# Cumulative sums along a diagonal: the sums of the last rows moved to TensorE, and the last places split over two PSUM tiles

## The chip, the cores and the metric

The kernel runs on one core of one Trainium2 chip. The metric is the device time of one execution in microseconds (us). Executions of the same kernel here spread over some 3.5 us (667.1 to 670.6), so differences of a few tenths of a microsecond are read from profiles, which time each instruction, and the timed runs tell only whether anything large has moved.

## The reference

```python
B, H, W = 4, 4224, 4224
x = randn(B, H, W).astype(float32)
ps = cumsum(cumsum(x, axis=1), axis=2)
diag = diagonal(ps, axis1=1, axis2=2)
out = cumsum(diag, axis=1).astype(float32)      # 4 x 4224
```

Each of the four matrices is read once (285 MB in all). The diagonal's element i is the sum of the leading (i+1) x (i+1) square, so it takes only row and column sums of the blocks on and beside the diagonal, and short scans of 384 places (11 groups make 4224).

## The kernel before

For each matrix, strips of 768 rows are loaded and converted to bf16. TensorE adds up columns into d (11 groups x 384), VectorE (DVE) and ScalarE (ACT) add up rows. The last matrix is treated apart, so that little is left to do when its last bytes land: the last group's rows come last, as part a (256 rows) in two loads, and part b (128 rows) in quarters, the last quarter in two loads. d and the scan of its groups are finished in the meantime. The sums of the last rows become places 0 to 383 of the last group (the code calls the row yl) by fp32 matmuls with a triangle of weights into the PSUM tile fin, called the weighing below; the last 32 places (ye) wait for the last quarter. In the code, arows are the sums of part a's rows, bsum those of the second and third quarter of part b, esum those of the last quarter; pu are the totals of d's groups, and carry is what each group adds from those before it.

Three helpers: `act_sum` adds up columns on ACT, `row_sums` and `pair_sum` on DVE, and `fold_in` lets TensorE add blocks of w columns into one PSUM tile by an identity matrix. The places concerned, at the last matrix:

```python
        for q in range(F2):
            matmul(d[:, q : GW : F2], r6[:, :NG, q], halves)
        for q in range(F):
            matmul(d[:, q : GW : F], r3[:, :, q], ident)

        if not whole:

            strip = strip_tile()
            part_a = strip[:, 0:2]
            part_b = strip[:, 2, :TB].rearrange("p (s c) -> p s c", s=4)
            acuts = [(1536, N - HC), (0, 1536)]
            for c0, c1 in acuts:
                nc.gpsimd.dma_start(out=part_a[:, :, c0:c1], in_=src_a[:, :, c0:c1])
            CB = TB // 4
            bcut = 768
            for sb, c0, c1 in (
                (0, 0, CB),
                (1, 0, CB),
                (2, 0, CB),
                (3, 0, bcut),
                (3, bcut, CB),
            ):
                r0 = TB + sb * R
                nc.gpsimd.dma_start(
                    out=part_b[:, sb, c0:c1],
                    in_=x[b, r0 : r0 + R, :TB].rearrange("r (k c) -> r k c", k=4)[
                        :, :, c0:c1
                    ],
                )

            fold_a = psum_s.tile([P, 2, 256], FP32, name="fold_a")
            c0, c1 = acuts[0]
            cp, ca = c0 + 768, c0 + 768 + 1152
            fold_in(fold_a, part_a, c0, cp, 256, start=True)
            for h in range(2):
                act_sum(asum[:, h, 1:2], part_a[:, h, cp:ca])
            row_sums(asum[:, :, 2], part_a[:, :, ca:c1])

        pu = smalls.tile([NG, 2], FP32, name="pu")
        c12 = smalls.tile([NG, 2, GW], FP32, name="c12")
        row_sums(pu[:, 0:1], d)
        masked(c12[:, 1, :], d, to_end, pu[:, 1:2])
        earlier, apart = order_whole if whole else order_last
        carry_ps = psum_s.tile([NG, 2], FP32, name="carry_ps")
        matmul(carry_ps, earlier, pu, start=True)
        matmul(carry_ps[:, 1:2], apart, pu[:, 0:1])
        carry = smalls.tile([NG, 2], FP32, name="carry")
        nc.vector.tensor_copy(out=carry, in_=carry_ps)
        for i, src in enumerate((d, c12[:, 0, :])):
            nc.vector.tensor_tensor_scan(
                out=c12[:, i, :],
                data0=ones_row,
                data1=src,
                initial=carry[:, i : i + 1],
                op0=ALU.mult,
                op1=ALU.add,
            )
        # ... store of groups 0 to 9; for the other matrices the loop ends here ...
        c0, c1 = acuts[1]
        cp = c0 + 768
        fold_in(fold_a, part_a, c0, cp, 256)
        for h in range(2):
            act_sum(asum[:, h, 3:4], part_a[:, h, cp:c1])
        row_sums(asum[:, :, 4], fold_a)
        arows = last.tile([P, 2], FP32, name="arows")
        row_sums(arows, asum)


        M0 = 2 * P
        E0 = GW - R
        fin = psum_s.tile([1, GW], FP32, name="fin")
        fin_e = psum_s.tile([1, R], FP32, name="fin_e")
        yl = last.tile([1, GW], FP32, name="yl")

        def weigh(rows, w, r0, start=False):

            matmul(fin[:, r0:], rows, w[:, : GW - r0], start=start)

        def finish(c0, c1):
            nc.vector.tensor_add(
                out=yl[:, c0:c1], in0=fin[:, c0:c1], in1=c12[0:1, 1, c0:c1]
            )

        by_ps = psum_s.tile([P, P], FP32, name="fold")
        for c in range(0, CB, P):
            matmul(by_ps, part_b[:, 0, c : c + P], weights4_h, start=c == 0)
        by = last.tile([P, P], FP32, name="by")
        nc.scalar.copy(out=by, in_=by_ps)
        weigh(dtot, weights, M0, start=True)
        weigh(ones_col, by, M0)
        weigh(arows[:, 0:1], weights, 0)
        weigh(arows[:, 1:2], weights, P)


        bsum = last.tile([P, 2, 2], FP32, name="bsum")
        for k, ca in ((0, 512), (1, 448)):
            act_sum(bsum[:, k, 0:1], part_b[:, k + 1, :ca])
            pair_sum(bsum[:, k, 1:2], part_b[:, k + 1, ca:])
        finish(0, M0)
        for k in range(2):
            for i in (1, 0):
                weigh(bsum[:, k, i : i + 1], weights4, M0 + (k + 1) * R)


        esum = last.tile([P, 3], FP32, name="esum")
        act_sum(esum[:, 0:1], part_b[:, 3, :320])
        pair_sum(esum[:, 1:2], part_b[:, 3, 320:bcut])
        pair_sum(esum[:, 2:3], part_b[:, 3, bcut:])
        for k in (1, 0, 2):
            matmul(fin_e, esum[:, k : k + 1], weights4[:, :R], start=k == 1)
        finish(M0, GW)
        nc.sync.dma_start(
            out=out[b, T0 : T0 + E0].unsqueeze(0), in_=yl[:, :E0]
        )
        ye = last.tile([1, R], FP32, name="ye")
        nc.vector.tensor_add(out=ye, in0=fin_e, in1=yl[:, E0:])
        nc.sync.dma_start(out=out[b, T0 + E0 : N].unsqueeze(0), in_=ye)
```

## Time and profile before

| | before |
|---|---|
| time, median of the first 3 runs | 667.89 us (667.13 to 668.78) |
| span of the profiled execution | 666.5 us |
| first columns of the last quarter landed (ACT starts on them) | 662.36 us |
| last store issued | 664.49 us |
| end of the span | 666.45 us |

Lines of the page's slices are tenths of busy time in 40 slices of the span. A timeline line is: start, duration, engine, line of the kernel, operation, output<-input, shapes, and in brackets the idle time of the engine before it and what ended that. The lines are shown in the prediction.

The granted clock is the profile's figure for TensorE, as a share of full speed. In the traces before and after it is 0.50 (half, also called cold) or 1.00 (full, warm) in each of 195 stretches of 3.41 us, and changes only between them; in the other traces the stretches asked for show the same two values. These stretches are called windows. The same four matmuls took 2.15 us at 0.50 (before) and 1.24 at 1.00 (b_again). Where the end of the program falls on this grid, the phase, differs from one execution to the next: the same kernel rose to full clock 3.37 us after the start of its last strip's fold in one (before) and 5.85 us in another (b_again).

One quantity carries this document: **the tail**, from the start of ACT's sum of 128x320, which begins as soon as the first columns of the last quarter have landed, to the issue of the last store. Before it is 664.49 - 662.36 = 2.13 us.

### The profile page before, as it was taken

What the parts mean: (1) busy time and instruction counts of PE and PEld (TensorE: products, weight loads), DVE (VectorE), ACT (ScalarE), POOL (GpSimd) and SP (SyncE); (2) the same over time, 40 slices, a digit from 0 to 9 for tenths busy, and PEclk for the clock granted to TensorE, in tenths of its full rate; (3) what the DMA queues carried; (4) which work ended last, traced back from release to release, by engine and by line L of the source; (5) the groups of instructions that cost most, each with busy time, mean ns of one, the idle gap of its engine ahead of it and who ended that gap; (6) DMA issues with size and microseconds to landing.
All of it is one profiled execution on the core that took longest, in us unless ns stands there. A gap on an engine that the chain in (4) does not pass through costs nothing.

```text
span 666.5 us, 2562 instructions
## 1 busy us (share of the span) xinstructions
PE 207.6 (31%) x981; PEld 98.5 (15%) x981; DVE 334.7 (50%) x165; ACT 140.3 (21%) x226; POOL 31.3 (5%) x59
## 2 busy tenths in 40 slices
PE   0081522403107154140321633504022254250426
PEld 0030211101103021010110311201011122120203
DVE  3160625446916153453882434537298334362866
ACT  0000120406300103040630020304063002030436
POOL 7000000000000000000000000000000000001000
PEclk9995857666558586665655957567565585765758
DMA  9999999999999999999999999999999999999997
GB/s 203 219 219 219 219 218 219 219 219 211 208 218 219 218 217 219 218 219 218 219 218 209 216 219 219 217 213 219 219 218 219 217 212 218 219 220 211 214 211 150
DMA packets 7670, 143.23 MB, mean 215 GB/s; under 512 B 702, under 2 KB 1002, under 8 KB 2154
## 3 DMA queue, kind: packets, MB, share of 16 engines
q0 software_dynamic: 7296, 142.47, 99.8%
q1 hardware_dynamic: 362, 0.61, 0.3%
q8 instruction: 7, 0.11, 0.1%
q14 instruction: 5, 0.04, 0.0%
HBM read 285.47 MB, written 0.07 MB: 428 GB/s over the span
## 4 chain that ended last, share of the span: by engine, by line
DVE 48%; another core or an unknown queue 44%; DMA 5%; PE 2%; issue 1%; DVEq 0%; POOLq 0%
DVE acc L254 29%; DVE mu L347 8%; DVE strip L348 8%; DMA strip<-in_x_dram 5%; DVE c L464 1%; PE d L208 1%; DVE parts L254 1%; PE fin L208 1%; DVE pu L254 0%; DVE c L274 0%; DVE acc L363 0%; DVE rows L388 0%; PE carry_ps L208 0%; PE fold L208 0%
## 5 line engine op out<-in xcount | busy, mean ns | idle before, releaser
L249 ACT ACTIVATE dump<-strip 128x416 bf16<-128x416 bf16 (+8 forms) x112 | 128.4, 1146 | 521.5 <-DMA strip<-in_x_dram 518.7
L347 DVE TENSOR_TENSOR mu<-strip,um 128x4608 bf16<-128x4608 bf16 (+1 forms) x24 | 52.4, 2183 | 307.0 <-DMA strip<-in_x_dram 306.8
L254 DVE TENSOR_REDUCE acc<-strip 128x6 f32<-128x4608 bf16 (+6 forms) x23 | 196.0, 8523 | 0.8
L208 PE MATMUL d<-strip,sel 128*11 128x384 bf16 x102 | 42.1, 413 | 375.1 <-DMA strip<-in_x_dram 375.1
L215 PEld LDWEIGHTS <-sel 128*11 128x11 bf16 x703 | 72.2, 103 | 502.1 <-issue 468.8
L215 PE MATMUL d<-strip,sel 128*11 128x384 bf16 x501 | 132.1, 407 | 0.0
L348 DVE TENSOR_TENSOR strip<-strip,mu 128x4608 bf16<-128x4608 bf16 (+1 forms) x24 | 52.4, 2183 | 1.0
L215 PE MATMUL d<-mu,sel 128*11 128x384 bf16 x200 | 43.6, 350 | 0.0
L76 POOL DMA_DIRECT2D strip<-in_x_dram x24 | 16.5, 687 | 542.8 <-DVE acc L254 279.8
L208 PE MATMUL d<-mu,sel 128*11 128x384 bf16 x43 | 15.5, 361 | 45.9 <-DVE mu L347 45.9
L249 ACT ACTIVATION_READ_ACCUMULATOR dump<-strip 128x1 f32 x112 | 20.9, 186 | 0.0
L208 PEld LDWEIGHTS <-sel 128*11 128x11 bf16 x146 | 14.7, 101 | 18.9 <-issue 10.3
L208 PE MATMUL d<-ident,rows 128*11 128x128 f32 x24 | 5.2, 379 | 17.5 <-DVE rows L397 16.8
L94 DVE MEMSET um<- 128x4608 bf16 (+1 forms) x2 | 4.9, 2458 | 1.1 <-issue 1.1
L208 PEld LDWEIGHTS d<-ident,rows 128*11 128x11 f32 x24 | 2.5, 118 | 19.4 <-DVE rows L397 11.7
L208 PE MATMUL d<-halves,rows 128*11 128x64 f32 x48 | 5.3, 290 | 0.0
L95 POOL TENSOR_SCALAR_AFFINE_SELECT um<-um 128x4608 bf16<-128x4608 bf16 (+1 forms) x2 | 5.2, 2612 | 2.4 <-DVE um L94 2.4
L208 PEld LDWEIGHTS d<-halves,rows 128*11 128x11 f32 x48 | 4.8, 130 | 1.2 <-issue 1.1
L254 DVE TENSOR_REDUCE pu<-d 11x1 f32<-11x384 f32 x4 | 2.2, 546 | 5.1 <-PE d L208 5.1
L464 DVE TENSOR_TENSOR_SCAN c<-ones_row,carry,c 11x384 f32<-11x384 f32 x4 | 4.0, 1005 | 0.1
L464 DVE TENSOR_TENSOR_SCAN c<-ones_row,carry,d 11x384 f32<-11x384 f32 x4 | 4.0, 1000 | 0.1
L437 POOL DMA_DIRECT2D strip<-in_x_dram x5 | 2.7, 557 | 26.4 <-DMA strip<-in_x_dram 26.4
(94 smaller groups left out, 48.2 us busy)
## 6 DMA issues: line engine op xcount, KB each, us to landing
strip<-in_x_dram POOLq DMA_DIRECT2D x19, 6336.0 KB, 76.6
strip<-in_x_dram POOLq DMA_DIRECT2D x5, 3168.0 KB, 59.7
strip<-in_x_dram POOLq DMA_DIRECT2D x1, 1080.0 KB, 49.9
strip<-in_x_dram POOLq DMA_DIRECT2D x1, 768.0 KB, 52.9
strip<-in_x_dram POOLq DMA_DIRECT2D x3, 256.0 KB, 54.1
head<-in_x_dram SPq DMA_DIRECT2D x1, 528.0 KB, 3.7
strip<-in_x_dram POOLq DMA_DIRECT2D x1, 192.0 KB, 43.2
strip<-in_x_dram POOLq DMA_DIRECT2D x1, 64.0 KB, 28.6
```

The lines of the kernel that those rows point to most:

```text
L76: nc.gpsimd.dma_start(out=o, in_=x[b, r0 : r0 + f * P, :].rearrange("(p f) w -> p f w", f=f))
L94: nc.vector.memset(um, 1.0)
L95: nc.gpsimd.affine_select(out=um, in_=um, compare_op=ALU.is_gt, fill=0.0, base=0, pattern=[[-1, f], [1, f * P]], channel_multiplier=-f,)
L208: nc.tensor.matmul(o, lhsT=lhsT, rhs=rhs, start=start, stop=False, skip_group_check=True)
L215: te.add_instruction(mybir.InstMatmult(start_tensor_calc=False, stop_tensor_calc=False, tile_position=(0, 0), tile_size=(P, P if lhsT.shap ...
L249: nc.scalar.activation(out=dump[:, :w], in_=src, func=ACT.Copy, accum_out=acc)
L254: nc.vector.reduce_sum(out=acc, in_=src, axis=AX.X)
L347: nc.vector.tensor_mul(out=mu, in0=block, in1=um)
L348: nc.vector.tensor_sub(out=block, in0=block, in1=mu)
L437: nc.gpsimd.dma_start(out=part_b[:, sb, c0:c1], in_=x[b, r0 : r0 + R, :TB].rearrange("r (k c) -> r k c", k=4)[:, :, c0:c1],)
L464: nc.vector.tensor_tensor_scan(out=c12[:, i, :], data0=ones_row, data1=src, initial=carry[:, i : i + 1], op0=ALU.mult, op1=ALU.add,)
```

## The change

The intent: TensorE, busy for only 31% of the span before, takes over the summing of part a from ACT and DVE (DVE keeps one sum over the 512 folded columns), with the matmuls put where it would otherwise wait; the scanned row is added by TensorE into the same PSUM tiles, so no addition of 384 places is left for DVE; places 0 to 255 and 256 to 383 lie in two tiles, so that the first can be copied and stored while the second is still written (as it then ran: DVE's copy from 662.12 to 662.53 us, passes of arows and bsum into the second from 661.92 on); and at the end only the addition of 32 places remains.

```diff
--- before.py
+++ after.py
@@ -238,10 +238,11 @@
     def fold_in(o, src, c0, c1, w, start=False):
 
         for c in range(c0, c1, w):
+            e = min(c + w, c1)
             if c == c0:
-                matmul(o, ident_h, src[..., c : c + w], start=start)
+                matmul(o[..., : e - c], ident_h, src[..., c:e], start=start)
             else:
-                matmul_on(o, ident_h, src[..., c : c + w])
+                matmul_on(o[..., : e - c], ident_h, src[..., c:e])
 
     def act_sum(acc, src):
         w = src.shape[-1]
@@ -295,7 +296,7 @@
         nc.vector.memset(rows3[i], 0.0)
 
 
-    asum = last.tile([P, 2, 5], FP32, name="asum")
+    asum = last.tile([P, 2, 2], FP32, name="asum")
     dtot = last.tile([P, 1], FP32, name="dtot")
     hs = last.tile([P, 3], FP32, name="hs")
     hu = last.tile([P, 3], FP32, name="hu")
@@ -411,11 +412,6 @@
             row_sums(parts[:, :, 2], fold_g)
             row_sums(r3[:, row_of(LG - 1), :], parts)
 
-        for q in range(F2):
-            matmul(d[:, q : GW : F2], r6[:, :NG, q], halves)
-        for q in range(F):
-            matmul(d[:, q : GW : F], r3[:, :, q], ident)
-
         if not whole:
 
             strip = strip_tile()
@@ -443,12 +439,18 @@
 
             fold_a = psum_s.tile([P, 2, 256], FP32, name="fold_a")
             c0, c1 = acuts[0]
-            cp, ca = c0 + 768, c0 + 768 + 1152
-            fold_in(fold_a, part_a, c0, cp, 256, start=True)
-            for h in range(2):
-                act_sum(asum[:, h, 1:2], part_a[:, h, cp:ca])
-            row_sums(asum[:, :, 2], part_a[:, :, ca:c1])
-
+            fcuts = [c0, c0 + 768, c0 + 2048, c1]
+
+        def fold_part(i):
+            if not whole:
+                fold_in(fold_a, part_a, fcuts[i], fcuts[i + 1], 256, start=i == 0)
+
+        for q in range(F2):
+            matmul(d[:, q : GW : F2], r6[:, :NG, q], halves)
+        fold_part(0)
+        for q in range(F):
+            matmul(d[:, q : GW : F], r3[:, :, q], ident)
+        fold_part(1)
 
         pu = smalls.tile([NG, 2], FP32, name="pu")
         c12 = smalls.tile([NG, 2, GW], FP32, name="c12")
@@ -458,6 +460,7 @@
         carry_ps = psum_s.tile([NG, 2], FP32, name="carry_ps")
         matmul(carry_ps, earlier, pu, start=True)
         matmul(carry_ps[:, 1:2], apart, pu[:, 0:1])
+        fold_part(2)
         carry = smalls.tile([NG, 2], FP32, name="carry")
         nc.vector.tensor_copy(out=carry, in_=carry_ps)
         for i, src in enumerate((d, c12[:, 0, :])):
@@ -478,65 +481,70 @@
             continue
 
 
-        c0, c1 = acuts[1]
-        cp = c0 + 768
-        fold_in(fold_a, part_a, c0, cp, 256)
-        for h in range(2):
-            act_sum(asum[:, h, 3:4], part_a[:, h, cp:c1])
-        row_sums(asum[:, :, 4], fold_a)
-        arows = last.tile([P, 2], FP32, name="arows")
-        row_sums(arows, asum)
-
-
         M0 = 2 * P
         E0 = GW - R
-        fin = psum_s.tile([1, GW], FP32, name="fin")
+        fin_a = psum_s.tile([1, M0], FP32, name="fin_a")
+        fin_b = psum_s.tile([1, P], FP32, name="fin_b")
         fin_e = psum_s.tile([1, R], FP32, name="fin_e")
         yl = last.tile([1, GW], FP32, name="yl")
-
-        def weigh(rows, w, r0, start=False):
-
-            matmul(fin[:, r0:], rows, w[:, : GW - r0], start=start)
-
-        def finish(c0, c1):
-            nc.vector.tensor_add(
-                out=yl[:, c0:c1], in0=fin[:, c0:c1], in1=c12[0:1, 1, c0:c1]
-            )
-
-
-
+        ye = last.tile([1, R], FP32, name="ye")
+
+        def weigh_a(rows, w, start=False):
+
+            matmul(fin_a, rows, w[..., :M0], start=start)
+
+        def weigh_b(rows, w, r0=0, start=False):
+
+            matmul(fin_b[:, r0:], rows, w[..., : P - r0], start=start)
+
+
+        c0, c1 = acuts[1]
+        fold_in(fold_a, part_a, c0, c1, 256)
         by_ps = psum_s.tile([P, P], FP32, name="fold")
         for c in range(0, CB, P):
             matmul(by_ps, part_b[:, 0, c : c + P], weights4_h, start=c == 0)
         by = last.tile([P, P], FP32, name="by")
         nc.scalar.copy(out=by, in_=by_ps)
-        weigh(dtot, weights, M0, start=True)
-        weigh(ones_col, by, M0)
-        weigh(arows[:, 0:1], weights, 0)
-        weigh(arows[:, 1:2], weights, P)
+        weigh_b(dtot, weights, start=True)
+        weigh_a(ones_col[0:1], c12[0:1, 1, :], start=True)
+        weigh_b(ones_col[0:1], c12[0:1, 1, M0:])
+
+
+        row_sums(asum[:, :, 1], fold_a)
+        arows = last.tile([P, 2], FP32, name="arows")
+        nc.vector.tensor_add(out=arows, in0=asum[:, :, 0], in1=asum[:, :, 1])
+        weigh_b(ones_col, by)
+        weigh_a(arows[:, 0:1], weights)
+        matmul(fin_a[:, P:], arows[:, 1:2], weights[:, :P])
+        weigh_b(arows[:, 0:1], weights[:, M0:])
+        weigh_b(arows[:, 1:2], weights[:, P:])
 
 
         bsum = last.tile([P, 2, 2], FP32, name="bsum")
-        for k, ca in ((0, 512), (1, 448)):
-            act_sum(bsum[:, k, 0:1], part_b[:, k + 1, :ca])
-            pair_sum(bsum[:, k, 1:2], part_b[:, k + 1, ca:])
-        finish(0, M0)
-        for k in range(2):
-            for i in (1, 0):
-                weigh(bsum[:, k, i : i + 1], weights4, M0 + (k + 1) * R)
-
-
         esum = last.tile([P, 3], FP32, name="esum")
+        act_sum(bsum[:, 0, 0:1], part_b[:, 1, :512])
+        pair_sum(bsum[:, 0, 1:2], part_b[:, 1, 512:])
+        for i in (1, 0):
+            weigh_b(bsum[:, 0, i : i + 1], weights4, R)
+        nc.vector.tensor_copy(out=yl[:, :M0], in_=fin_a)
+        nc.sync.dma_start(
+            out=out[b, T0 : T0 + M0].unsqueeze(0), in_=yl[:, :M0]
+        )
+        act_sum(bsum[:, 1, 0:1], part_b[:, 2, :448])
+        pair_sum(bsum[:, 1, 1:2], part_b[:, 2, 448:])
+        for i in (1, 0):
+            weigh_b(bsum[:, 1, i : i + 1], weights4, 2 * R)
+
+
         act_sum(esum[:, 0:1], part_b[:, 3, :320])
         pair_sum(esum[:, 1:2], part_b[:, 3, 320:bcut])
         pair_sum(esum[:, 2:3], part_b[:, 3, bcut:])
+        nc.scalar.copy(out=yl[:, M0:], in_=fin_b)
+        nc.sync.dma_start(
+            out=out[b, T0 + M0 : T0 + E0].unsqueeze(0), in_=yl[:, M0:E0]
+        )
         for k in (1, 0, 2):
             matmul(fin_e, esum[:, k : k + 1], weights4[:, :R], start=k == 1)
-        finish(M0, GW)
-        nc.sync.dma_start(
-            out=out[b, T0 : T0 + E0].unsqueeze(0), in_=yl[:, :E0]
-        )
-        ye = last.tile([1, R], FP32, name="ye")
         nc.vector.tensor_add(out=ye, in0=fin_e, in1=yl[:, E0:])
         nc.sync.dma_start(out=out[b, T0 + E0 : N].unsqueeze(0), in_=ye)
```

## The prediction

> **What bounds the kernel now.** I read the page first, its slices and its queue table, and asked what runs nearly all the time.
>
> ```profile
> PE   0081522403107154140321633504022254250426
> PEclk9995857666558586665655957567565585765758
> DMA  9999999999999999999999999999999999999997
> ```
>
> The reader is to see that the row of the DMA engines is full (9) in 39 of 40 slices, while TensorE is nearly idle in many; the page gives 142.47 MB for the input queue and 99.8% of the engines' time. The kernel before is bound by its reads over the whole span. The changed lines all belong to the last matrix, and most of them run after its last big strip. So I went to that end: first the windows of 3.41 us between two steps of the granted clock (columns: PE, weight loads, DVE, ACT, POOL busy with counts; clock; DMA share; GB/s), then the timeline.
>
> ```profile
> 648.66:652.07 3.41, 3.37 (x9) 1.07 (x9) 3.25 (x3) 3.26 (x5) 0.00 (x0) 0.50 1.06 215
> 652.07:655.49 3.42, 2.67 (x25) 1.72 (x26) 2.96 (x5) 2.98 (x5) 0.00 (x0) 1.00 1.06 211
> 655.49:658.90 3.41, 1.82 (x12) 0.66 (x11) 2.92 (x6) 2.27 (x5) 0.00 (x0) 1.00 1.09 207
> 658.90:662.31 3.41, 3.41 (x16) 1.27 (x15) 1.86 (x7) 2.27 (x7) 0.00 (x0) 0.50 0.96 170
> 662.31:665.73 3.42, 1.23 (x16) 0.76 (x14) 1.39 (x7) 0.56 (x2) 0.00 (x0) 1.00 0.00 0
> ```
>
> Input arrives at about 210 GB/s until some 662 us and then stops. TensorE was busy 1.82 of 3.41 us in the window from 655.49, and after it the clock fell to 0.50 for just the window in which the last sums are weighed. Then the timeline, from the first weighing to the end:
>
> ```profile
> 660.50 2.15 PE L208 MATMUL fin<-weights,arows 128*1 128x384 f32 x4
> ...
> 662.36 0.47 ACT L249 ACTIVATE dump<-strip 128x320 bf16<-128x320 bf16 x1 [0.30 <-DMA strip<-in_x_dram]
> 662.68 0.41 DVE L502 TENSOR_TENSOR yl<-fin,c 1x256 f32<-1x256 f32 x1 [0.89 <-PE fin L208]
> 662.74 0.19 ACT L249 ACTIVATION_READ_ACCUMULATOR dump<-strip 128x1 f32 x1
> 663.02 0.37 DVE L263 SCALAR_TENSOR_TENSOR pair<-strip 128x224 f32<-128x224 bf16 x1
> ...
> 663.15 0.71 PE L208 MATMUL fin<-weights,bsum 128*1 128x96 f32 x8 [0.50 <-DVE yl L502]
> ...
> 663.33 0.28 DVE L263 SCALAR_TENSOR_TENSOR pair<-strip 128x128 f32<-128x128 bf16 x1
> ...
> 663.70 0.34 PE L208 MATMUL fin_e<-weights,esum 128*1 128x32 f32 x6
> 663.90 0.28 DVE L502 TENSOR_TENSOR yl<-fin,c 1x128 f32<-1x128 f32 x1 [0.28 <-PE fin L208]
> ...
> 664.28 0.18 DVE L540 TENSOR_TENSOR ye<-fin_e,yl 1x32 f32<-1x32 f32 x1
> 664.49 0.24 SPq L541 DMA_DIRECT2D out_dram<-ye  x1
> ```
>
> The first columns of the last quarter of part b (128x320 on ACT, 128x224 pairs on DVE) had landed at about 662.33, where ACT could start (the rest landed soon after, as no input moves past 662.5), but DVE stood 0.89 us in front of the addition of places 0 to 255, which waited for the four slow matmuls of arows. It reached its 224 columns only at 663.02: 0.7 us lost. TensorE in turn waited for that addition before it could write fin again. From the last issue (664.49) to the end (666.45) are 1.96 us, which the change does not touch.
>
> [...] every step of the clock lies on such a grid and only 0.5 and 1.0 occur. In this trace cold windows at least 0.83 busy were followed by a full clock and one at 0.75 was not; warm windows at 0.45 or more kept it, those at 0.39 or less lost it, with the one at 0.53 (above) between. [...] here 512 columns of the fold started about 0.22 us apart at full clock, and an fp32 matmul is two passes, a 384-column pass taking 0.64 us cold, so half of it, 0.32, warm. [...] the additions on places 0 to 255 held up matmuls into places 288 and on of the same tile for 0.50 us. [...]
>
> **The change part by part.**
> *Fold of part a.* Before, 6 matmuls of 512 columns fold part of a; ACT took four sums (two of 1.16 and two of 0.84 us, each with a 0.19 read: 4.8 us), DVE one of 0.65. After, the first 2160 columns take 3 + 5 full matmuls and one of 224, the other 1536 take 6: 14.4 matmul units for 6. Extra: 8.4 x 0.22 = 1.9 us warm, 3.6 cold. ACT and DVE were not the limit at that place (ACT was idle before each landing), so the 4.8 and 0.65 us are mostly off the path. Three matmuls go in front of the last sums into d: part a had landed at 653.9, so 3 x 0.22 ends at 654.55, and the rows they must not delay are ready at 654.54. Five more end at about 656.4, and the carry's matmul was issued at 656.6. So 0 to 0.1 us on the path when warm, about 1 us if cold.
> *Scanned row by matmul and split tiles.* fp32 columns weighed before: 128 + 128 + 384 + 256 = 896, after: 128 + 256 + 128 + 128 + 256 + 128 + 128 + 128 = 1280, two passes each. That is 384 x 2 / 1.2 = 0.64 us more warm, 1.3 cold. Removed from DVE: the addition of 0.28 between the last matmul into fin and ye; ACT copies that row instead, beside DVE.
> *Clock.* The five to nine matmuls more between 655.5 and 658.9 lift TensorE's share there from 0.53 to about 0.85, an estimate from the 0.22 us each, so the clock should stay full in the next window. Then, from the landing at 657.56: six folds to 658.9, by to 659.6, dtot and the two row matmuls (two passes each, 0.21 + 0.43 + 0.21) to 660.4, by 660.6, arows of fin_a 0.64 to 661.2. DVE's copy of fin_a ends near 661.8, before the last data has landed. DVE then takes the third quarter's 0.54 and the last two pair sums of 0.44 and 0.35, which end about 663.05 for 663.61 before. fin_e + 0.25 = 663.3, ye 663.4 to 663.55, issue 663.56. That is **0.9 us earlier** than 664.49 for this profile.
> *Store of 0 to 255 alone.* One more issue on SP (about 0.23 us, near 661.8) when SP is idle: no cost.
>
> **Discount.** [...] another execution has another phase. I went through phases by hand with the busy times above: the kernel before loses its clock in the weighing in about 40% of them; in the others arows ends near 661.6 and the gain is only about 0.1 us. So the mean gain is 0.4 x 0.9 + 0.6 x 0.1 = 0.42, and some more from the 0.28 addition taken off the path in phases between; I say 0.65. 667.89 - 0.65 is about **667.2 us**.
>
> **The rivals.**
> (a) TensorE becomes the bound of the tail. If the clock stays at half, 14.4 units and 1280 fp32 columns take it from 657.56 past 664.5 before fin_a is done, and DVE's copy, which stands ahead of two pair sums, holds everything: about 1.5 to 2 us slower, 669.5. For it: the clock fell in this trace. Against it: the added work is itself what keeps TensorE busy. Chance 1 in 8.
> (b) Nothing moves: the end is set by the last landing plus the chain pair sum, fin_e, ye, store, and the waits removed were mostly hidden in other executions. Time 667.7 to 667.9. Chance 1 in 4.
> (c) The reads shift: not likely, since the buffers, their release and all issues of input are the same; the extra store is 1 KB of 142 MB.
>
> **Range and chances.** The three runs before spread over 1.65 us, which I take as 0.6 us of error in a median; with 0.5 for the gain I get 0.8, so 8 in 10 lie within about 0.9: 666.3 to 668.1. Two per cent are 13.4 us, while all of the tail after the last landing is only 4 us; so within 2% has 0.985, faster 0.005, slower 0.01.
>
> **What would show it.** In the changed profile: DMA full as before until some 662 us after the start; a clock of 1.0 through the window of the weighing; fin_a copied before the last landing; no DVE wait for TensorE of over 0.3 us ahead of the last two pair sums; last issue about 1.3 us after the last landing (before: 664.49 less 662.33, 2.2 us). It would be wrong if the clock is 0.5 there, if fold matmuls push pu or the carry by over 0.5 us, or if the copy of fin_a ends after 662.5.

What is cut from it are general statements for which no trace of this case was given. The forecast's sum came to 667.89 - 0.65 = 667.2 us, the 0.65 raised from 0.4 x 0.9 + 0.6 x 0.1 = 0.42; none of its terms is cut. Its unit times are read from the trace before: the folds of 512 columns started 0.22 us apart at full clock (655.35, 655.57), those of 480 columns 0.40 us apart at half clock (649.06, 649.46), so that 8.4 units at half clock are some 3.6 us, an estimate from the latter. Passes of 384 fp32 columns started 0.64 us apart at half clock (660.50, 661.14, 661.78); half of that, 0.32 us or 1.2 columns per ns at full clock, is an estimate, and it is the divisor in 384 x 2 / 1.2 and behind 0.21, 0.43 and 0.64. In the changed kernel the four passes of arows into fin_a, 768 columns in all, took 0.65 us from the first start to the start of the next pass (661.27 to 661.92).

That the clock should stay full at a share of 0.85 rests on the trace before alone, where every full window with a share of 0.58 or more was followed by another; what decides the clock was not shown. The shares given for losing it leave out the first 34 us, where ten idle windows stand at 1.00. The 40% is the author's estimate, by hand.

## The result, and the profile after

| | before | after |
|---|---|---|
| median, 6 runs each, all of the fast state | 668.34 us (667.13 to 670.6) | 667.67 us (667.33 to 669.91) |
| span profiled | 666.5 us | 666.1 us |
| ACT's sum of 128x320 starts | 662.36 us | 662.94 us |
| last store issued | 664.49 us | 664.14 us |
| tail | 2.13 us | 1.20 us |

The ratio of after to before is 0.9991, 95% interval 0.997 to 1.0011: the same time. (It is given as recorded; the ratio of the medians is 0.9990.) The medians differ by 0.67 us, but the interval reaches from 2.0 us faster to 0.7 us slower, so the timing alone shows nothing. The profiles do. The row of the DMA engines of the changed kernel is as full as before:

```profile
DMA  9999999999999999999999999999999999999998
```

The windows of the changed kernel between steps of the clock (busy us and counts of PE, weight loads, DVE, ACT, POOL; then the clock, DMA share and GB/s):

```profile
652.71:656.13 3.42, 3.34 (x28) 1.99 (x27) 2.31 (x4) 1.41 (x2) 0.00 (x0) 1.00 1.07 212
656.13:659.54 3.41, 2.94 (x18) 1.20 (x17) 2.92 (x6) 0.00 (x0) 0.00 (x0) 1.00 1.09 208
659.54:662.95 3.41, 3.31 (x29) 1.77 (x27) 2.25 (x9) 1.67 (x6) 0.00 (x0) 1.00 0.94 166
```

TensorE is now busy 2.94 of 3.41 us in the window that had 1.82, and the window in which the weighing runs has a clock of 1.00 in place of 0.50. The timeline of the end:

```profile
661.27 0.81 PE L208 MATMUL fin_a<-weights,arows 128*1 128x256 f32 x4
...
662.12 0.41 DVE L529 COPY yl<-fin_a 1x256 f32<-1x256 f32 x1 [1.04 <-PE fin_a L208]
...
662.88 0.39 DVE L264 SCALAR_TENSOR_TENSOR pair<-strip 128x224 f32<-128x224 bf16 x1
662.94 0.47 ACT L250 ACTIVATE dump<-strip 128x320 bf16<-128x320 bf16 x1 [0.26 <-DMA strip<-in_x_dram]
...
663.20 0.29 DVE L264 SCALAR_TENSOR_TENSOR pair<-strip 128x128 f32<-128x128 bf16 x1
...
663.33 0.50 PE L208 MATMUL fin_e<-weights,esum 128*1 128x32 f32 x6
...
663.94 0.18 DVE L548 TENSOR_TENSOR ye<-fin_e,yl 1x32 f32<-1x32 f32 x1 [0.44 <-PE fin_e L208]
664.14 0.23 SPq L549 DMA_DIRECT2D out_dram<-ye  x1
```

DVE still waits for TensorE, 1.04 us ahead of its copy of fin_a, but it is back from that copy at 662.53, takes the third quarter's 288 columns, and reaches the 224 columns at 662.88, no later than ACT its part of the same load; before, it came 0.7 us late. The span became shorter by only 0.36 us because in this execution the reads ended 0.58 us later: +0.58 - 0.93 (tail) - 0.01 (closing).

The two profiles also happen to have met nearly the same phase of the clock's windows: the clock rose 3.37 us after the start of the last strip's fold before (648.70 to 652.07) and 3.42 us after (649.29 to 652.71). So they can be compared directly: with the same phase the kernel before lost its clock and the changed one kept it. What TensorE does more in the window from 656.13 is the fold of part a alone, for the weighing into the split tiles starts only at 660.01. So of the parts of the change it is the fold that can have kept the clock, if it is TensorE's work in that window that keeps it, which is the theory.

### The profile page after: what moved, and what is told of

Read it like the earlier page. It is cut to its first block, busy times and chain, and to the rows that moved or that the text cites. A ratio compares the mean times of both kernels' runs of the same rounds, so it can differ in the third digit from the quotient of the medians.

```text
span 666.1 us, 2585 instructions
## 1 busy us (share of the span) xinstructions
PE 209.2 (31%) x998; PEld 99.5 (15%) x998; DVE 333.8 (50%) x163; ACT 136.1 (20%) x219; POOL 31.3 (5%) x59
## 3 DMA queue, kind: packets, MB, share of 16 engines
q0 software_dynamic: 7296, 142.47, 99.9%
## 4 chain that ended last, share of the span: by engine, by line
DVE 44%; another core or an unknown queue 41%; DMA 13%; PE 2%; issue 1%; DVEq 0%; POOLq 0%
DVE acc L255 27%; DMA strip<-in_x_dram 13%; DVE mu L348 7%; DVE strip L349 7%; DVE c L467 1%; PE d L208 1%; PE fold_a L215 0%; DVE pu L255 0%; DVE c L275 0%; PE fold_a L208 0%; PE fin_b L208 0%; PE fin_a L208 0%; DVE acc L364 0%; DVE rows L389 0%
## 5 line engine op out<-in xcount | busy, mean ns | idle before, releaser
L250 ACT ACTIVATE dump<-strip 128x416 bf16<-128x416 bf16 (+6 forms) x108 | 124.4, 1151 | 520.8 <-DMA strip<-in_x_dram 518.1
L76 POOL DMA_DIRECT2D strip<-in_x_dram x24 | 16.5, 688 | 543.4 <-DVE acc L255 281.4
L215 PEld LDWEIGHTS <-ident_h 128*128 128x128 bf16 x18 | 2.1, 114 | 13.7 <-issue 12.7
```

Of the source, the lines that this page charges most:

```text
L76: nc.gpsimd.dma_start(out=o, in_=x[b, r0 : r0 + f * P, :].rearrange("(p f) w -> p f w", f=f))
L215: te.add_instruction(mybir.InstMatmult(start_tensor_calc=False, stop_tensor_calc=False, tile_position=(0, 0), tile_size=(P, P if lhsT.shap ...
L250: nc.scalar.activation(out=dump[:, :w], in_=src, func=ACT.Copy, accum_out=acc)
```

## The experiments

Theory: the tail is long where TensorE loses its full clock just before the weighing, because the slow matmuls then hold up DVE; the fold keeps TensorE busy enough. Rivals: the order of the work and the shared tile cost the time at any clock; or TensorE's added work is itself a cost. The edits are shown shortened. In all, 12 runs; all results were correct, all timed runs of state fast, the single looks of unknown state. "Rise" is the time from the start of the last strip's fold to the step to full clock. "Busy before" is TensorE's busy time in the window before the one that holds most of the passes of arows (into fin, or fin_a where there are two tiles).

| kernel | rise, us | busy before, us | clock in the weighing | tail, us |
|---|---|---|---|---|
| before | 3.37 | 1.82 | 0.5 | 2.13 |
| b_again | 5.85 | 2.56 | 1.0 | 1.14 |
| warm | 4.71 | 3.20 | 1.0 | 1.31 |
| fold_only | 5.83 | 2.95 | 1.0 | 1.87 |
| fold_again | 4.68 | 3.35 | 1.0 | 1.29 |
| late_add | 4.55 | 2.19 | 1.0 | 1.40 |
| late_again | 2.99 | 2.09 | 1.0 | 1.35 |
| no_fold | 3.89 | 1.79 | 0.5 | 3.29 |
| no_fold_again | 5.88 | 2.60 | 1.0 | 1.20 |
| after | 3.42 | 2.94 | 1.0 | 1.20 |
| a_again | 3.24 | 2.94 | 1.0 | 1.21 |
| row_add | 5.19 | 2.99 | 1.0 | 1.21 |
| one_store | 3.38 | 2.93 | 1.0 | 1.21 |
| warm_start | full before it | 2.91 | 1.0 | 1.21 |

The two executions with 1.82 us or less of work in that window had half clock in the weighing; the twelve with 2.09 or more had full clock. With the work of the kernel before on TensorE, the clock was kept at rises of 2.99, 4.55, 5.85 and 5.88 us and lost at 3.37 and 3.89. So only executions with a rise near 3.4 test what the fold does for the clock: before (3.37, lost) against after, one_store and a_again (3.42, 3.38 and 3.24, kept).

### b_again: the kernel before, unchanged, profiled once more

> The kernel before, unchanged, for a second profile: how much of its tail is the phase of the clock's windows. Tail here and below: from the start of ACT's sum of 128x320 (first columns of the last quarter, landed) to the issue of the last store; it was 2.13 us before and 1.20 us in the changed kernel. If the phase is free, this run has another one: with a full clock during the arows matmuls the tail is about 1.3 us, with half clock again about 2.1. If the tail is 2.1 at full clock, the clock is not the cause.

This execution had another phase. Its windows and the end of its timeline:

```profile
655.93:659.34 3.41, 2.56 (x23) 1.46 (x21) 2.31 (x6) 2.23 (x5) 0.00 (x0) 1.00 1.10 210
659.34:662.75 3.41, 2.76 (x18) 0.87 (x16) 2.58 (x7) 2.51 (x8) 0.00 (x0) 1.00 1.03 184
```

```profile
661.68 1.24 PE L208 MATMUL fin<-weights,arows 128*1 128x384 f32 x4
...
663.66 0.39 DVE L263 SCALAR_TENSOR_TENSOR pair<-strip 128x224 f32<-128x224 bf16 x1 [0.22 <-DMA strip<-in_x_dram]
663.72 0.47 ACT L249 ACTIVATE dump<-strip 128x320 bf16<-128x320 bf16 x1 [0.34 <-DMA strip<-in_x_dram]
...
664.86 0.23 SPq L541 DMA_DIRECT2D out_dram<-ye  x1
```

The same four matmuls take 1.24 us in place of 2.15, which is 0.91 of the 0.99 us by which the tail is shorter; DVE waits for the landing and not for TensorE, and the tail is 1.14 us, shorter even than the 1.20 of the changed kernel. The kernel before is not slow by its order of work; it is slow at its end in some executions. The single time, 668.51 us, is long all the same, because the reads ended late (663.72).

### warm: eight matmuls without use

```diff
             matmul(d[:, q : GW : F], r3[:, :, q], ident)
+        if not whole:
+            idle_ps = psum_s.tile([P, 512], FP32, name="idle_ps")
+            for k in range(5):
+                matmul(idle_ps, ident_h, um6[:, 0, :512], start=k == 0)
@@
         fold_in(fold_a, part_a, c0, cp, 256)
+        for k in range(3):
+            matmul(idle_ps, ident_h, um6[:, 0, :512])
```

> The kernel before plus eight matmuls of 512 columns on constants into an unused PSUM tile (five after the last sums into d, three after the second fold of part a); nothing else changes. Theory clock: TensorE's share in the window before the weighing rises above 0.7, the clock stays 1.0, the four arows passes take 1.1 us instead of 2.15, VectorE's wait for TensorE before the addition of places 0 to 255 falls from 0.89 to under 0.2 us, and the tail is 1.3 to 1.5 us. Rival order (shared tile and the addition ahead of the pair sums are what costs, at any clock): the tail stays at 1.9 to 2.1 us.

TensorE was busy 3.16 and 3.20 us of the two windows from 655.07, the clock stayed at 1.0, the four arows passes took 1.24 us, DVE had no wait before the addition of places 0 to 255, and the tail was 1.31 us (664.02 to 665.33). Ratio to before 1.0002 (0.9986 to 1.0019). It fits the clock, but proves less than it seems: this execution rose at 4.71 us, not at the 3.37 at which the kernel before lost its clock, and b_again kept the clock without the extra matmuls.

### no_fold and no_fold_again: the changed kernel with ACT and DVE summing part a

```diff
-            fcuts = [c0, c0 + 768, c0 + 2048, c1]
-        def fold_part(i): ...        # and its three calls
+            cp, ca = c0 + 768, c0 + 768 + 1152
+            fold_in(fold_a, part_a, c0, cp, 256, start=True)
+            for h in range(2):
+                act_sum(asum[:, h, 1:2], part_a[:, h, cp:ca])
+            row_sums(asum[:, :, 2], part_a[:, :, ca:c1])
@@
-        fold_in(fold_a, part_a, c0, c1, 256)
+        cp = c0 + 768
+        fold_in(fold_a, part_a, c0, cp, 256)
+        for h in range(2):
+            act_sum(asum[:, h, 3:4], part_a[:, h, cp:c1])
```

> The changed kernel with the sums of part a put back to ACT and VectorE; two PSUM tiles, row by matmul and own store stay. Theory clock: with TensorE's share near 0.5 in the window before the weighing the clock drops to 0.5, the 1280 fp32 columns then take 4.3 us instead of 2.1, the copy of fin_a ends after 663.5 and the tail is 2.2 to 3.5 us, longer than before. If the clock happens to stay 1.0, 1.2 us. Rival order: tail 1.2 to 1.4 us whatever the clock.

The first execution met half clock. Its windows, then its timeline:

```profile
656.20:659.61 3.41, 1.79 (x17) 0.95 (x17) 2.92 (x6) 2.24 (x6) 0.00 (x0) 1.00 1.11 209
659.61:663.02 3.41, 3.41 (x13) 1.09 (x13) 0.87 (x4) 2.19 (x8) 0.00 (x0) 0.50 0.77 135
663.02:666.44 3.42, 2.51 (x20) 1.79 (x17) 1.49 (x8) 0.34 (x2) 0.00 (x0) 0.50 0.00 0
```

```profile
662.55 0.47 ACT L250 ACTIVATE dump<-strip 128x320 bf16<-128x320 bf16 x1 [0.34 <-DMA strip<-in_x_dram]
...
663.33 0.41 DVE L529 COPY yl<-fin_a 1x256 f32<-1x256 f32 x1 [2.66 <-PE fin_a L208]
...
665.84 0.23 SPq L549 DMA_DIRECT2D out_dram<-ye  x1
```

TensorE's share in the window before was 1.79 of 3.41, the clock fell, DVE stood 2.66 us in front of the copy of fin_a, and the tail was 3.29 us, 1.2 more than before. Two things differ here: the new form weighs more columns (1280 in place of 896), and the clock stayed at 0.50 to the end, though TensorE was busy through all of the window from 659.61, while before it was full again from 662.31. How much each costs was not separated. So without its fold the change can have the longer tail. Its ratio was 1.0016 (0.9999 to 1.0032), by verdict the same; five of its six timed runs lie between 669.51 and 669.95, which hints that half clock was common, but only profiled executions show the clock.

> The changed kernel without the fold, a second profile; the first met half clock (3.29 us). With a full clock in the weighing the clock theory says 1.2 us, as TensorE has less to do before it than in the changed kernel; at half clock again 3.0 to 3.5. If it is over 2 us at full clock, the extra weighing columns and not the clock are the cost.

The second execution kept the clock:

```profile
664.08 0.47 ACT L250 ACTIVATE dump<-strip 128x320 bf16<-128x320 bf16 x1 [0.25 <-DMA strip<-in_x_dram]
...
665.28 0.23 SPq L549 DMA_DIRECT2D out_dram<-ye  x1
```

A tail of 1.20 us, by the same program. The 2.09 us between the two executions go with the clock; at full clock the extra columns cost nothing that can be seen (b_again's tail, with 896, is 1.14).

### fold_only and fold_again: the kernel before with the fold alone

```diff
-            cp, ca = c0 + 768, c0 + 768 + 1152
-            fold_in(fold_a, part_a, c0, cp, 256, start=True)
-            ...                      # act_sum, row_sums of the first columns
+            fcuts = [c0, c0 + 768, c0 + 2048, c1]
+        def fold_part(i): ...        # called as in the change
@@
-        fold_in(fold_a, part_a, c0, cp, 256)
-        ...
+        fold_in(fold_a, part_a, c0, c1, 256)
+        row_sums(asum[:, :, 1], fold_a)
```

> The kernel before with part one alone of the change: TensorE folds all of part a; last places still in one PSUM tile, row added by VectorE, one store. Theory clock: this is enough, clock 1.0 in the weighing, tail 1.3 to 1.5 us, of the 0.93 us gained in the changed kernel at least 0.6. Rival order: tail 1.9 us or more.

The clock was 1.0 in the weighing, as expected, but the tail was 1.87 us: a miss for my theory in its simple form. The timeline shows why:

```profile
657.40 0.55 DVE L255 TENSOR_REDUCE pu<-d 11x1 f32<-11x384 f32 x1 [2.06 <-PE d L208]
...
663.11 0.47 ACT L250 ACTIVATE dump<-strip 128x320 bf16<-128x320 bf16 x1 [0.28 <-DMA strip<-in_x_dram]
663.17 0.41 DVE L502 TENSOR_TENSOR yl<-fin,c 1x256 f32<-1x256 f32 x1 [0.60 <-PE fin L208]
```

The clock rose only 5.83 us after the start of the strip's fold, so this fold and the sums into d ran cold, three folds of part a stood ahead of the last sums into d, and DVE waited 2.06 us for d. Carry, scan, arows and the addition all came that much later, and DVE reached the last columns late again. The kernel before at the same phase (b_again, 5.85 us) waited 0.65 us for d and had a tail of 1.14: at so late a rise, between these two executions, the fold in one tile cost 0.73 us.

> The kernel with the fold alone, a second profile for another phase. If its 1.87 us came from the late rise of the clock (655.35, after the fold of the last strip had run cold, so that d, carry and arows were late), a phase with the rise before 653 gives 1.2 to 1.5 us. If the shared tile and the place of the addition cost 0.5 us at any phase, it is 1.7 or more again, with VectorE waiting over 0.5 us before the addition of places 0 to 255.

The clock rose 4.68 us after the start. DVE's wait for d fell to 1.50 us and that ahead of the addition was gone:

```profile
656.83 0.55 DVE L255 TENSOR_REDUCE pu<-d 11x1 f32<-11x384 f32 x1 [1.50 <-PE d L208]
```

The tail was 1.29 us, in the expected range. At such a rise the kernel before kept its clock too (late_add, 4.55), so this run shows that the fold does little harm here, and that the shared tile does not cost 0.5 us at any phase; what the fold alone brings near a rise of 3.4 us was not run. Its ratio in the timed runs was 1.0007 (0.9992 to 1.0021).

### row_add: the changed kernel with DVE adding the scanned row

```diff
-        weigh_a(ones_col[0:1], c12[0:1, 1, :], start=True)
-        weigh_b(ones_col[0:1], c12[0:1, 1, M0:])
@@
-        nc.vector.tensor_copy(out=yl[:, :M0], in_=fin_a)
+        nc.vector.tensor_add(out=yl[:, :M0], in0=fin_a, in1=c12[0:1, 1, :M0])
@@  (after the matmuls into fin_e)
-        nc.scalar.copy(out=yl[:, M0:], in_=fin_b)
+        nc.vector.tensor_add(out=yl[:, M0:], in0=fin_b, in1=c12[0:1, 1, M0:])
```

> The changed kernel with the scanned row added by VectorE again (places 0 to 255 by an addition in place of the copy; places 256 to 383 by an addition between the last pair sums and ye), no row matmuls. Removes 768 fp32 column passes from TensorE (0.64 us warm) and puts 0.28 us back on VectorE ahead of ye, but beside fin_e (0.4 us). Theory phase: fin_a ready 0.6 us earlier relative to the landing where arows allows it, tail 1.2 to 1.4 us at full clock, that is, the row by matmul is worth 0 to 0.2 us. Rival (the addition at the end is what cost before): 1.5 us or more.

Tail 1.21 us (663.09 to 664.30), ratio 0.9999 (0.9976 to 1.0022). The row by matmul brings nothing that can be seen at this phase: the addition of 0.28 us (663.71 to 663.99) runs while TensorE still weighs the last quarter into fin_e (663.60 to 664.03). Its clock rose late, at 5.19 us, and the tail stayed short all the same, while fold_only at 5.83 us had 1.87. That speaks for the two tiles in such phases (only 384 fp32 columns are weighed ahead of the first addition, in place of 640), but 0.64 us lie between the two rises, so it is not shown.

### late_add and late_again: one addition at the end of the kernel before

```diff
-        finish(0, M0)
@@
-        finish(M0, GW)
+        finish(0, GW)
```

> The kernel before with its addition of places 0 to 255 taken out of the middle and one addition of all 384 places at the end; one tile, ACT and VectorE sums as before. Takes away both VectorE's wait for arows ahead of the pair sums and TensorE's wait for that addition, at any clock, and costs 0.54 instead of 0.28 us at the end. Theory order: tail 1.5 to 1.7 us even where the clock is 0.5. Theory clock: where the clock is 0.5 in the weighing it stays at 1.9 to 2.1 us, as the slow passes are still in front of bsum and fin_e; at full clock 1.3 to 1.5.

> The kernel before with one late addition, a second profile; the first met a full clock (1.40 us). If this one meets half clock in the weighing, theory order says 1.5 to 1.7 us and theory clock 1.9 to 2.1 us; at full clock 1.40 again.

Both executions kept a full clock, with tails of 1.40 us (664.61 to 666.01) and 1.35 (663.00 to 664.35). The question put to them, what the order does at half clock, stays open. At full clock the late addition of 384 places is 0.2 to 0.3 us worse than b_again's 1.14. The ratio was 1.0006 (0.9988 to 1.0023).

### warm_start: the changed kernel with a clock already full when the last strip lands

```diff
+            idle_ps = psum_s.tile([P, 512], FP32, name="carry_ps")
+            for k in range(32):
+                matmul(idle_ps, ident_h, um6[:, 0, :512], start=k == 0)
             fold_in(fold_g, strip[:, F:], 0, wp, 160, start=True)
```

> The changed kernel plus 32 matmuls of 512 columns on constants into a dead PSUM tile between 638 and 648 us, where TensorE otherwise idles: the clock is then full when the last big strip lands, whatever the phase. Theory phase: the folds of that strip run 0.22 us apart instead of 0.40, the carry comes at the time that DVE allows, DVE's wait for fin_a (1.04 us in the changed kernel, 0.5 us of it past the landing of the third quarter) shrinks below 0.6 us, and the tail is 1.0 to 1.2 us, close to the changed kernel's 1.20. Rival (TensorE's early clock has no part): same 1.2, wait unchanged.

The clock was 1.0 from 641.76 to the end, and the folds of that strip started about 0.2 us apart. But DVE's wait for fin_a was 1.02 us and the tail 1.21: the rival was right, the early clock has no part in it. By the time of the weighing the path runs from the landing of the second load of part a (657.85) through the six folds and TensorE's own row of passes to fin_a at 661.82 without a pause, and that does not start earlier. My expectation had also misread the wait of 1.04 us in the changed kernel: the third quarter, on which ACT starts at 662.01, had landed only 0.1 us before the wait ended, not 0.5. The ratio was 0.9994 (0.9977 to 1.001).

### one_store and a_again: the own store, and the changed kernel once more

```diff
-        nc.sync.dma_start(out=out[b, T0 : T0 + M0].unsqueeze(0), in_=yl[:, :M0])
@@
-            out=out[b, T0 + M0 : T0 + E0].unsqueeze(0), in_=yl[:, M0:E0]
+            out=out[b, T0 : T0 + E0].unsqueeze(0), in_=yl[:, :E0]
```

> The changed kernel with places 0 to 255 and 256 to 351 in one store again, behind the copy of fin_b. In the changed kernel the stores were issued at 662.56 and 663.67 us, the last one (ye) at 664.14, so the early store lies beside other work. Expected: tail 1.20 us as with two stores (between 1.15 and 1.25) at full clock. If the own store is what shortens the end, the tail grows by 0.1 us or more.

> The changed kernel, unchanged, for a second profile at whatever phase of the clock's windows it meets. Theory phase (the change makes the tail independent of the phase from the fold on, the kernel before is short when it keeps its clock and long when it loses it): tail from ACT's sum of 128x320 to the last store's issue 1.1 to 1.4 us, if the clock rises by 653 us; up to 1.7 if, as in the run with the fold alone, it rises only at 655 and the carry is late. Rival (the changed kernel's 1.20 was luck of the phase as much as the 2.13 of before): over 1.9 us.

Tails of 1.21 us in both (662.38 to 663.59, and 662.87 to 664.08). The own store is worth nothing that can be seen, and the changed kernel's short tail was not the luck of one execution: four executions with it or with small variations of it, at rises from 3.24 to 5.19 us, lie within 0.01 us of each other (after, a_again, one_store, row_add), and so does warm_start. A rise as late as 5.8 us, at which fold_only was slow, was not met with the changed kernel; there its tail is not known.

No version that the runs point to would beat both kernels by an amount that timing resolves: once the clock is full, tails lie between 1.14 and 1.40 us (1.87 in one), while the end of the reads moves by 2.25 us from one execution to the next (662.36 before, 664.61 in late_add).

## Why the prediction was right

The measured 667.67 us lies in the range 666.3 to 668.1, and within 2% was given 0.985. That says little of the mechanism: the range also holds 667.89, the time before on which it was built, so a change without any effect would have been in it. Step by step:

- **The reads set the span.** Right: the DMA row is as full (the input queue took 99.8% of the engines' time before, 99.9% after), and the span of both profiles is the end of the reads plus tail plus 1.95 us of closing.
- **The clock.** Right, and the main mechanism. TensorE's share went from 0.53 to 2.94/3.41 = 0.86 (predicted about 0.85), and the clock stayed full. The pairs before and b_again, no_fold and no_fold_again show the clock's worth within one program: 0.99 and 2.09 us. That the fold keeps it rests on one execution that lost it (before) and three that did not, at rises of 3.24 to 3.42 us. My reading that a share of 0.53 is what loses the clock is not borne out: other windows with as little kept it (last section).
- **The fold delays d and carry by 0 to 0.1 us.** Right at this phase: from the end of rows to pu 0.92 us before (654.53 to 655.45), 1.01 after (655.11 to 656.12). The "about 1 us if cold" showed in fold_only, where DVE waited 2.06 us for d.
- **The tail 0.9 us shorter for this profile.** 0.93 measured. The single steps were less exact: fin_a was ready 0.86 us before ACT's 128x320 (662.08 against 662.94), where I had 1.13 (661.2 against 662.33). It still came before the last data. By the letter my sign against it was met, as the copy of fin_a ended at 662.53 and I had named 662.5; but the reads of this execution ended 0.58 us later.
- **The phases.** I gave the kernel before 40% of executions with half clock in the weighing, an estimate. Of six profiles of kernels with its load on TensorE (before, b_again, late_add, late_again, no_fold, no_fold_again) two were such, and none of eight with more. Few, but not against it.
- **The discount.** Here a step was wrong, though it moved the result little. I raised 0.42 to 0.65 us for the addition of 0.28 us taken off the path. row_add puts it back at no cost (1.21 us), and b_again ends in 1.14 us with it in place; it lies beside the matmuls into fin_e. I had also put a gain of 0.1 us where the clock is full; it is 1.14 - 1.20 = -0.06 us. With the measured sizes, one third of 0.93 less two thirds of 0.06 is 0.27 us, an estimate from two profiles in six. The medians' 0.67 us agrees with the 0.65 that I predicted, but with a mean gain of about 0.27 us and an interval from -2.0 to +0.7 us that is luck, as far as these runs can tell.
- **The rivals.** (a), TensorE as the bound, is what no_fold shows (3.29 us); with the fold it was not met at the phases seen. (b), nothing moves, is true of the executions in which the kernel before keeps its clock, and the timed runs (667.67, the same) do not rule it out as a whole. (c) did not happen.
- **The signs.** I wrote that no wait of over 0.3 us for TensorE would lie ahead of the last two pair sums. One of 1.04 us is there, ahead of the copy, but most of it is time in which DVE had nothing landed to add; the pair sums themselves came at their landing.

Open: how often the kernel before loses its clock, since six profiles are few; the exact condition under which the clock falls; what order and tiles do at half clock; what the changed kernel does when the clock rises 5.8 us late; and the mean gain in time, which lies below what these runs resolve.

## What to carry to other kernels

Here more work on TensorE went with a faster next task: after 2.94 of 3.41 us busy the weighing met a clock of 1.00 (after), after 1.82 one of 0.50 (before), and the four passes of arows in the kernel before took 1.24 us at the one clock (b_again) and 2.15 at the other (before). That less work can make the next task slower is what no_fold suggests (1.79 us busy, then 0.50, and a tail of 3.29 us), though no_fold_again kept its clock. So look at the granted clock window by window before judging a shift of work by durations alone. Profile a kernel twice before explaining a gap of a microsecond: two executions of one program lay 0.99 us (before, b_again) and 2.09 us (no_fold, no_fold_again) apart in their tails, one with half clock in the weighing and one with full. In this kernel, with the DMA row full (9) in 39 of 40 slices, what is left to an edit of the sums is what follows the last landing, and that is a tail of 1 to 3 us (1.14 to 3.29), with 2 us of closing (1.96 before, 1.95 after), of 667.

## What the traces show of the clock, the fp32 passes and the last store

- The clock fell after windows that were far from idle: 1.82 us busy of 3.41 (before, from 655.49) and 1.79 (no_fold, from 656.20). It stayed full after 1.58 of 3.42 (before, from 211.76) and 1.78 of 3.42 (warm_start, from 652.00), so the busy time that the profile shows is not by itself the measure. In the traces before and after, eight full windows with a share between 0.45 and 0.60 kept the clock (five and three), and one, at 0.53, lost it. Why that one and the one of no_fold, at 0.52, is open.
- A window with 3.00 of 3.41 us busy was followed by the rise to full clock (late_again, from 649.03), one with 2.46 was not (no_fold_again, from 649.58), and once a window busy throughout was not either (no_fold, from 659.61: the clock was 0.50 in the next). What raises it is open too.
- Each fp32 matmul is two passes here (the two matmuls of arows are four in the timeline before), and passes of 384 columns started 0.64 us apart at half clock (660.50, 661.14, 661.78); the four passes into fin, 1280 columns in all, took 2.15 us at half (before) and 1.24 us at full clock (b_again).
- The last store of 128 bytes, issued by SyncE, completed 1.04 us after its issue before (664.49 to 665.53) and 1.03 after (664.14 to 665.17); the rest of the 1.96 us to the end before was the program's closing.
